# Feed-forward block products: the fifth product's operand added up in the first one's SBUF buffer for three of five double groups, instead of in DRAM

## The chip, the cores and the metric

The kernel runs on one core of a Trainium2 chip. A core has a matrix engine (PE, with its weight loads shown as PEld), a vector engine (DVE), an activation engine (ACT), a general engine (POOL) and a queue engine (SP) that does nothing here but issue transfers. Each engine takes its instructions in program order and waits at semaphores. Transfers run on 16 shared DMA engines: those that SP issues go through one queue (q1 in the profile), those that POOL issues through another (q0). Only POOL issues transfers that add to what lies at their destination.

The metric is the device time of one execution in microseconds, as the median of some runs.

## What is computed

One layer of a decoder over 256 tokens of width 1024: rotary attention in blocks beside an HGRN2 recurrence, a gated merge, cross-attention to 256 memory tokens, and at its end a feed-forward block of hidden width 2816. The change is in how the weights of the last part are brought in:

```python
hn = rmsnorm(h, norm_ffn_g[l])
gu = hn @ w_ffn_in[l]
h = h + (jax.nn.silu(gu[..., :FFN_HIDDEN]) * gu[..., FFN_HIDDEN:]) @ w_ffn_out[l]
...
return rmsnorm(h, final_norm_g)
```

## The kernel before, in words

**Matmuls.** All weights lie in DRAM as units of 128x2048 float32 (1 MB). A unit is loaded into SBUF ("raw"), split by ACT into a rounded part ("hi", two halves of 128x1024) and by DVE into the rest ("lo"), and PE multiplies three times (hi by hi, hi by lo, lo by hi). Up to the feed-forward part `prep` does this (load L254, hi L261, lo L265), two units ahead of PE, with three "raw" buffers that go round; PE takes a unit in `gemm_f` (L338, L339) or `gemm_t` (L317 to L319).

**Feed-forward.** The hidden width has eleven slices of 256 columns. Ten of them are taken as five double groups, q = 1, 3, 5, 7, 9 (slices q and q+1), each with seven products instead of eight, after Strassen's scheme (Winograd's form). The four weight blocks of a group are called 11, 21, 12 and 22. The products, in the order in which PE takes them:

- P1 uses block 11, P2 block 21
- P6 uses 11 + 12 + 22, P7 uses 12 + 22, P5 uses 11 + 12
- P3 uses block 22
- P4 uses 11 + 12 + 21 + 22, up to signs that the tokens' side carries

A product (`ffn_product`, L1143) is 12 matmuls. Between products stand the output matmuls of earlier slices ("O" units, `ffn_out`, 24 matmuls). `FFN_PLAN` is the order of all 48 units. In it a group's P1 to P5 read P1, P2, O, P6, P7, P5 for q = 3, 5 and 7, then follow O, P3, P4 and the next group's P1.

**Where the sums are made.** `block_sums` makes them in DRAM long before, in steps: one step goes by with each matmul unit of the first two thirds, and the table `SUMS` gives the step of each. For each group SP copies a block within DRAM and POOL adds another block to it with an accumulating transfer:

- t3 = 22 (SP, L830), then t3 += 12 (POOL, L819): the operand of P7
- t1 = 11 (SP, L831), then t1 += 12 (POOL): the operand of P5
- t2 = t3 (SP, L834), then t2 += 11 (POOL): the operand of P6

The copy of t3 into t2 must wait for the addition into t3 to land. These transfers are held in program order on SP and POOL (`keep_in_program_order`). SP's loads of the weights of the earlier stages stand in the same row, so whatever SP waits for, the loads behind it wait for too.

P4's operand of groups 3 to 9 is made in another way: P2's block stays in its SBUF buffer (B12 or B6), and once it is split, POOL adds P6's sum to it there (L1413). `operand` then hands the same buffer to P4.

**Feed-forward loads.** `prep_u` brings units in up to four ahead of the one that PE takes: `operand` or `fetch` issues the load (SP, L1388; L1395 for P2's block), `halve` splits it (ACT L1374, DVE L1382). `fetch` takes buffers in the order of `raws`: three "raw" buffers and, from the eleventh load on, B10 and B11 in turn with them ("rawx"). The split parts lie in three hi and three lo buffers and one fixed pair (px), so a unit is split once PE is through with the unit some four places earlier.

Of the kernel before, what the change touches and what calls it, by code (L numbers as in the profile page):

```python
# [12 lines left out]
F32 = mybir.dt.float32  # L13
# [3 lines left out]
ALU = mybir.AluOpType  # L17
# [74 lines left out]
def ffn_plan():  # L92
# [10 lines left out]
    for q in (3, 5, 7):  # L103
# [4 lines left out]

FFN_PLAN = ffn_plan()
DOUBLES = (1, 3, 5, 7, 9)  # L110
PINNED = (5, 6)
FIRST = [0, 4, 1, 2, 3]
SUMS = {1: (0, 4, 2, 6, 10, 13), 3: (7, 9, 8, 11, 17, 20), 5: (13, 15, 16, 18, 26, 28), 7: (22, 25, 29, 31, 32, 34),
        9: (33, 36, 46, 51, 48, None)}
HOME = (36, 38)
T4 = (19, 23)
TURNS = {6: (0,), 10: (1,), 12: (2,), 19: (3,), 21: (4,), 28: (5,), 30: (6,), 38: (7,), 41: (8,)}
# [53 lines left out]
def build(tc, A, out):  # L171
    nc = tc.nc
    V, SC, G, PE, SY = nc.vector, nc.scalar, nc.gpsimd, nc.tensor, nc.sync
    with ExitStack() as ctx:
# [8 lines left out]
        dr = pool("dr", 1, space=bass.MemoryType.DRAM)  # L183
# [3 lines left out]
        def big(tag, name, shape=(128, 8, 256), dt=F32):  # L187
            return bp.tile(list(shape), dt, name=name, tag=tag)
# [31 lines left out]
        made, at = [0], [0]  # L220
# [590 lines left out]
        scr = {}  # L811

        def block(q, name):
            i, kh = {"11": (1, 0), "21": (1, 1), "12": (0, 0), "22": (0, 1)}[name]
            return A["w"][where["T", "wkv_x", 1024 + 512 * (1 - i), kh] if q == "vx" else where["I", q + i, kh]]

        def block_sums():
            def add(t, q, name):
                tc.keep_in_program_order(G.dma_start(t, block(q, name), accum_op=ALU.add, max_dma_last_dim=8192))  # L819

            steps = {}

            def at_step(i, f):
                steps.setdefault(i, []).append(f)

            for q in DOUBLES:
                t1, t2_, t3 = (dr.tile([128, 2048], F32, name="%s_%s" % (z, q)) for z in ("t1", "t2", "t3"))
                scr[q] = {"P5": t1, "P6": t2_, "P7": t3}
                at = SUMS[q]
                at_step(at[0], lambda t=t3, q=q: tc.keep_in_program_order(SY.dma_start(t, block(q, "22"))))  # L830
                at_step(at[2], lambda t=t1, q=q: tc.keep_in_program_order(SY.dma_start(t, block(q, "11"))))  # L831
                at_step(at[1], lambda t=t3, q=q: add(t, q, "12"))
                at_step(at[3], lambda t=t1, q=q: add(t, q, "12"))
                at_step(at[4], lambda t=t2_, t3=t3: tc.keep_in_program_order(SY.dma_start(t, t3)))  # L834
                if q != DOUBLES[-1]:
                    at_step(at[5], lambda t=t2_, q=q: add(t, q, "11"))
                if q == DOUBLES[0]:
                    t4 = dr.tile([128, 2048], F32, name="t4")
                    scr[q]["P4"] = t4
                    at_step(T4[0], lambda t=t4, t2_=t2_: tc.keep_in_program_order(SY.dma_start(t, t2_)))  # L840
                    at_step(T4[1], lambda t=t4, q=q: add(t, q, "21"))
            def home():
                sums["3"] = big("B6", "b22", (128, 2048))
                SY.dma_start(sums["3"], block("vx", "22"))

            at_step(HOME[0], home)
            at_step(HOME[1], lambda: G.dma_start(sums["3"], block("vx", "12"), accum_op=ALU.add))
            for i in range(max(steps) + 1):
                for f in steps.get(i, ()):
                    f()  # L850
                yield 1
# [431 lines left out]
        def last_sum():  # L1283
            tc.keep_in_program_order(G.dma_start(scr[DOUBLES[-1]]["P6"], block(DOUBLES[-1], "11"), accum_op=ALU.add,
                                                 max_dma_last_dim=8192))
# [63 lines left out]


        px = big("P1", "px", (128, 4096), F32R)
        made_u, pair, blk = [0], {}, {}
        homes = itertools.cycle(("B12", "B6"))
        raws = itertools.chain((None,) * 6 + ("B6", None, "B12", None), itertools.cycle(("B10", "B11", None, None, None)))

        PAIRS = [None, None, None, "px", ("B7", "B14"), ("B10", "B11")]

        def halve(raw, n):
            def pin(z):
                if n in PINNED:  # L1360
                    tc.keep_in_program_order(z)

            tags = PAIRS[n] if n < 6 else PAIRS[n % 4 + 2 if n % 4 == 1 else 0]
            if tags == "px":
                hi, lo = px[:, 0:2048], px[:, 2048:4096]
            elif tags:
                hi, lo = (big(tag, name, (128, 2048), F32R) for tag, name in zip(tags, ("hix", "lox")))
            else:
                hi = wh.tile([128, 2048], F32R, name="hi", tag="hi")
                lo = wl.tile([128, 2048], F32R, name="lo", tag="lo")  # L1370
            for c in range(2):
                a = slice(c * 1024, (c + 1) * 1024)
                with tc.issue_after(turned_v[3] if n == 0 else squared[1]) if n == 0 or (n, c) == (3, 1) else nullcontext():
                    pin(SC.activation(hi[:, a], raw[:, a], AF.Copy))  # L1374
            pieces = 2 if n < 3 else 1
            w = 2048 // pieces
            for c in range(pieces):
                a = slice(c * w, (c + 1) * w)
                with ExitStack() as then:
                    for ins in behind.get(n, ()) if (n, c) != (2, 1) else (added[1],):  # L1380
                        then.enter_context(tc.issue_after(ins))
                    pin(V.tensor_tensor(lo[:, a], raw[:, a], hi[:, a].bitcast(F32), op=ALU.subtract))  # L1382
            return hi, lo
# [8 lines left out]
        def operand(q, name):  # L1392
            if name == "P2" and q != DOUBLES[0]:
                blk[q] = big(next(homes), "b21", (128, 2048))
                tc.keep_in_program_order(SY.dma_start(blk[q], block(q, "21")))  # L1395
                return blk[q]
            if name == "P4" and q in blk:
                return blk.pop(q)
            return fetch(scr[q][name] if name in scr[q] else block(q, {"P1": "11", "P2": "21", "P3": "22"}[name]))
# [3 lines left out]
        def prep_u(upto):  # L1403
            while made_u[0] <= min(upto, len(units) - 1):
                n = FIRST[made_u[0]] if made_u[0] < len(FIRST) else made_u[0]
                if n == 20:
                    SY.dma_start(gfin, A["gfin"].to_broadcast([128, 1024]))
                made_u[0] += 1
                u = units[n]
                raw = operand(u[1], u[2]) if u[0] == "P" else fetch(A["w"][where[u]])  # L1410
                pair[n] = halve(raw, n)
                if u[0] == "P" and u[1] in blk and u[2] == "P2":
                    G.dma_start(raw, scr[u[1]]["P6"], accum_op=ALU.add)  # L1413

# [181 lines left out]
        for n in range(4, len(units) - 2):  # L1596
# [6 lines left out]
            u = units[n]  # L1603
# [123 lines left out]
```

## Time and profile before

| what | before |
|---|---|
| median of 3 runs | 592.38 us (592.34 to 592.53) |
| the profiled execution: time | 592.17 us |
| the profiled execution: span of its instructions | 590.2 us |
| its granted TensorE clock | 0.998 |
| PE busy | 582.3 us |
| DVE busy | 452.5 us |
| ACT busy | 389.5 us |
| POOL busy | 122.5 us |
| moved by transfers | 161.92 MB |

The span is the time from the first instruction to the last; 1.97 us of the profiled execution's time lie around it. "Busy" counts an engine's instructions but not its waits and not the issuing of transfers. In lists of waits, "A <- B" says that A stood still until B was done. For a transfer the profile gives the time from its issue to its landing.

### The profile page before, as it was taken

Reading aid. Unit: us, or ns where it says so; the run is one execution under the profiler, and the core shown is the slowest. Engines: PE = TensorE matmul, PEld = TensorE weight load, DVE = VectorE, ACT = ScalarE, POOL = GpSimd, SP = SyncE. Lnnn points to the kernel's source line nnn. Section 1 sums busy time; section 2 is a strip of 40 time slices with the busy share of each in tenths; the row PEclk is TensorE's granted clock in tenths of the full one; section 3 lists DMA queues with packets and bytes.
Section 4 is the critical chain, followed back from the end, with each engine's and each line's share of the span. In section 5 each row is a group of like instructions: output and inputs, shape, how many; then the busy total and the mean of one; then the engine's idle time right before and its main releaser. Section 6 shows DMA issues by size and latency. Waiting matters only on the chain.

```text
span 590.2 us, 9030 instructions
## 1 busy us (share of the span) xinstructions
PE 582.3 (99%) x3474; PEld 487.9 (83%) x3474; DVE 452.5 (77%) x638; ACT 389.5 (66%) x638; POOL 122.5 (21%) x139
## 2 busy tenths in 40 slices
PE   9999999999999999999999999999999999999995
PEld 6888888888888888888888888888888888888884
DVE  6598967789858775858868785987878887877943
ACT  7795646555677566657548676776858676776743
POOL 2897300243301430003202332200000000000003
PEclk9999999999999999999999999999999999999999
DMA  9877997489996799899976986886989969796601
GB/s 337 339 273 290 274 343 310 144 277 354 325 308 243 210 299 333 264 403 276 256 242 184 372 268 237 212 283 245 366 289 294 408 180 421 200 418 190 236 1 71
DMA packets 22586, 161.92 MB, mean 274 GB/s; under 512 B 2832, under 2 KB 3472, under 8 KB 5392
## 3 DMA queue, kind: packets, MB, share of 16 engines
q1 hardware_dynamic: 18368, 135.35, 58.1%
q0 software_dynamic: 3456, 25.17, 21.8%
q10 hardware_dynamic: 720, 0.84, 0.4%
q8 instruction: 27, 0.44, 0.3%
q14 instruction: 15, 0.12, 0.1%
HBM read 160.29 MB, written 34.60 MB: 330 GB/s over the span
## 4 chain that ended last, share of the span: by engine, by line
PE 92%; DVE 3%; ACT 1%; issue 1%; POOL 1%; DMA 1%; DVEq 0%; POOLq 0%; ACTq 0%
PE psf L338 13%; PE pqA L1143 11%; PE pst L317 9%; PE pst L318 8%; PE pst L319 8%; PE psf L339 6%; PE pqF L1143 6%; PE acc L317 3%; PE acc L319 3%; PE acc L318 3%; PE pqB L1143 3%; DVE lo L265 2%; PE psg L593 1%; PE pso L318 1%; PE pso L319 1%
## 5 line engine op out<-in xcount | busy, mean ns | idle before, releaser
L265 DVE TENSOR_TENSOR lo<-raw,hi 128x1024 fp32r<-128x1024 f32 (+1 forms) x126 | 156.8, 1262 | 39.4 <-ACT hi L261 39.1
L261 ACT ACTIVATE hi<-raw 128x1024 fp32r<-128x1024 f32 (+1 forms) x126 | 126.5, 1027 | 56.6 <-PE pst L319 25.9
L338 PE MATMUL psf<-XX,hi 128*128 128x512 f32 x192 | 68.5, 401 | 0.0
L317 PE MATMUL pst<-hi,XX 128*128 128x512 f32 x160 | 63.7, 398 | 0.0
L319 PE MATMUL pst<-hi,XX 128*128 128x512 f32 x160 | 62.5, 390 | 0.0
L318 PE MATMUL pst<-lo,XX 128*128 128x512 f32 x160 | 62.4, 390 | 0.0
L339 PE MATMUL psf<-XX,lo 128*128 128x256 f32 x192 | 54.0, 281 | 0.0
L1382 DVE TENSOR_TENSOR lo<-raw,hi 128x2048 fp32r<-128x2048 f32 (+1 forms) x19 | 37.0, 1951 | 10.6 <-ACT hi L1374 10.5
L338 PEld LDWEIGHTS psf<-XX,hi 128*128 128x128 f32 x192 | 36.1, 188 | 8.7
L1374 ACT ACTIVATE hi<-raw 128x1024 fp32r<-128x1024 f32 x32 | 32.0, 1051 | 7.3 <-PE acc L319 5.3
L339 PEld LDWEIGHTS psf<-XX,lo 128*128 128x128 f32 x192 | 36.4, 189 | 0.0
L317 PEld LDWEIGHTS pst<-hi,XX 128*128 128x128 f32 x160 | 30.1, 188 | 7.3 <-issue 1.0
L319 PEld LDWEIGHTS pst<-hi,XX 128*128 128x128 f32 x160 | 30.0, 188 | 6.4
L318 PEld LDWEIGHTS pst<-lo,XX 128*128 128x128 f32 x160 | 30.1, 188 | 5.8
L1382 DVE TENSOR_TENSOR lo<-rawx,hi 128x2048 fp32r<-128x2048 f32 x12 | 27.5, 2288 | 7.6 <-ACT hi L1374 7.6
L1413 POOL DMA_DIRECT2D b<-t x4 | 3.5, 884 | 123.4 <-DVE fu L1476 88.1
L1374 ACT ACTIVATE hi<-rawx 128x1024 fp32r<-128x1024 f32 x24 | 24.1, 1050 | 4.8 <-DMA rawx<-w 1.8
L1143 PE MATMUL pqA<-hi,SS 128*128 128x512 f32 x80 | 26.4, 391 | 0.0
L317 PE MATMUL acc<-hi,hids 128*128 128x512 f32 x62 | 24.5, 395 | 0.0
L319 PE MATMUL acc<-hi,hids 128*128 128x512 f32 x62 | 24.2, 390 | 0.0
L318 PE MATMUL acc<-lo,hids 128*128 128x512 f32 x62 | 24.2, 390 | 0.0
L338 PE MATMUL psf<-H,hi 128*128 128x512 f32 x64 | 22.8, 400 | 0.0
(470 smaller groups left out, 1506.2 us busy)
## 6 DMA issues: line engine op xcount, KB each, us to landing
raw<-w SPq DMA_DIRECT2D x74, 1024.0 KB, 7.8
t<-w POOLq DMA_DIRECT2D x16, 1024.0 KB, 12.8
raw<-t SPq DMA_DIRECT2D x12, 1024.0 KB, 7.9
rawx<-w SPq DMA_DIRECT2D x10, 1024.0 KB, 7.5
b<-w SPq DMA_DIRECT2D x6, 1024.0 KB, 8.8
b<-w POOLq DMA_DIRECT2D x4, 1024.0 KB, 9.2
rawx<-t SPq DMA_DIRECT2D x4, 1024.0 KB, 7.8
b<-t POOLq DMA_DIRECT2D x4, 1024.0 KB, 9.4
```

Of the source, the lines that this page charges most:

```text
L261: SC.activation(hi[:, a], raw[:, a], AF.Copy)
L265: V.tensor_tensor(lo[:, a], raw[:, a], hi[:, a].bitcast(F32), op=ALU.subtract)
L317: PE.matmul(ps, xh, h, start=first, stop=False)
L318: PE.matmul(ps, xh, l, start=False, stop=False)
L319: PE.matmul(ps, xl, h, start=False, stop=last)
L338: PE.matmul(ps, w[0][:, k, a], X2[:, :, k], start=k == 0, stop=False)
L339: PE.matmul(ps[:, 0], w[1][:, k, a], X2[:, 0, k], start=False, stop=k == 7)
L593: PE.matmul(pss[c][t], z[:, k, t * 128:(t + 1) * 128], ws[c][0][:, k], start=z is Xh and k == 0, stop=False)
L1143: PE.matmul(ps, x[k], z[:, k], start=first and k == 0 and i == 0, stop=k == 3 and i == 2, skip_group_check=not first)
L1374: pin(SC.activation(hi[:, a], raw[:, a], AF.Copy))
L1382: pin(V.tensor_tensor(lo[:, a], raw[:, a], hi[:, a].bitcast(F32), op=ALU.subtract))
L1413: G.dma_start(raw, scr[u[1]]["P6"], accum_op=ALU.add)
```

## The change

For q = 3, 5 and 7 (`GROWN`), t1 is no longer made in DRAM: one copy of SP and one addition of POOL fall away for each. The first product's block 11 is loaded into buffer B10 (for q = 3, 5, 7 and 9). Once it is split for P1, POOL issues a transfer that adds block 12 to it in that buffer, and P5 takes its operand from there, with no load of its own. For q = 1 and q = 9, P5's operand is made in DRAM as before. B10 leaves the turn of the other loads: from the eleventh on they have four buffers instead of five.

`SUMS` is written in another order of columns. For q = 1 and 9 its steps are the same. For q = 3 the copy of t3 into t2 moves from step 17 to 11 and the addition to t2 from 20 to 17; for q = 5 from 26 to 18 and from 28 to 26; for q = 7 the copy from 32 to 31.

```diff
+GROWN = (3, 5, 7)
...
-SUMS = {1: (0, 4, 2, 6, 10, 13), 3: (7, 9, 8, 11, 17, 20), 5: (13, 15, 16, 18, 26, 28), 7: (22, 25, 29, 31, 32, 34),
-        9: (33, 36, 46, 51, 48, None)}
+SUMS = {1: (0, 4, 10, 13, 2, 6), 3: (7, 9, 11, 17), 5: (13, 15, 18, 26), 7: (22, 25, 31, 34),
+        9: (33, 36, 48, None, 46, 51)}
...
-                t1, t2_, t3 = (dr.tile([128, 2048], F32, name="%s_%s" % (z, q)) for z in ("t1", "t2", "t3"))
-                scr[q] = {"P5": t1, "P6": t2_, "P7": t3}
+                t2_, t3 = (dr.tile([128, 2048], F32, name="%s_%s" % (z, q)) for z in ("t2", "t3"))
+                scr[q] = {"P6": t2_, "P7": t3}
                 at = SUMS[q]
                 at_step(at[0], lambda t=t3, q=q: tc.keep_in_program_order(SY.dma_start(t, block(q, "22"))))
-                at_step(at[2], lambda t=t1, q=q: tc.keep_in_program_order(SY.dma_start(t, block(q, "11"))))
                 at_step(at[1], lambda t=t3, q=q: add(t, q, "12"))
-                at_step(at[3], lambda t=t1, q=q: add(t, q, "12"))
-                at_step(at[4], lambda t=t2_, t3=t3: tc.keep_in_program_order(SY.dma_start(t, t3)))
+                if q not in GROWN:
+                    t1 = scr[q]["P5"] = dr.tile([128, 2048], F32, name="t1_%s" % q)
+                    at_step(at[4], lambda t=t1, q=q: tc.keep_in_program_order(SY.dma_start(t, block(q, "11"))))
+                    at_step(at[5], lambda t=t1, q=q: add(t, q, "12"))
+                at_step(at[2], lambda t=t2_, t3=t3: tc.keep_in_program_order(SY.dma_start(t, t3)))
                 if q != DOUBLES[-1]:
-                    at_step(at[5], lambda t=t2_, q=q: add(t, q, "11"))
+                    at_step(at[3], lambda t=t2_, q=q: add(t, q, "11"))
...
-        raws = itertools.chain((None,) * 6 + ("B6", None, "B12", None), itertools.cycle(("B10", "B11", None, None, None)))
+        raws = itertools.chain((None,) * 6 + ("B6", None, "B12", None), itertools.cycle(("B11", None, None, None)))
...
+            if name == "P1" and q != DOUBLES[0]:
+                early[q] = big("B10", "b11", (128, 2048))
+                SY.dma_start(early[q], block(q, "11"))
+                return early[q]
+            if name == "P5" and q in GROWN:
+                return early[q]
...
                 pair[n] = halve(raw, n)
+                if u[0] == "P" and u[1] in GROWN and u[2] == "P1":
+                    G.dma_start(raw, block(u[1], "12"), accum_op=ALU.add)
```

The rows below show what the change moves. They name a transfer by its tiles, out<-in ("w" is the weights' array), and in brackets the semaphores it waits for: DMASW stands for the landing of one of POOL's transfers, DMAHW for that of one of SP's, the rest for engines.

The first place is SP's row in the stage of the first projections, some 120 to 165 us into the span. Before:

```order
L830 DMA t3_5_723<-w 16x16384
L254 DMA raw_1599<-w 128x2048 [waits DMAHW7_49,DMAHW3_49,DVE_49]
L254 DMA raw_1673<-w 128x2048 [waits DMAHW0_49,DVE_49]
L254 DMA raw_1790<-w 128x2048 [waits DMAHW1_49,DVE_49]
L831 DMA t1_5_721<-w 16x16384 [waits DMAHW6_49]
L254 DMA raw_1835<-w 128x2048 [waits DMAHW3_49,DVE_49]
L834 DMA t2_3_719<-t3_3_720 16x16384 [waits DMASW2_49]
L254 DMA raw_1880<-w 128x2048 [waits DMAHW4_49,DVE_49]
L254 DMA raw_1935<-w 128x2048 [waits DMAHW5_49,DMAHW2_49,DVE_49]
L840 DMA t4_717<-t2_1_715 16x16384 [waits DMASW4_49]
L254 DMA raw_2051<-w 128x2048 [waits DMAHW7_49,DVE_49]
```

And the same stretch of SP's row with the change:

```order
L831 DMA t3_5_721<-w 16x16384 [waits DMAHW1_49]
L837 DMA t2_3_718<-t3_3_719 16x16384 [waits DMASW2_49]
L255 DMA raw_1595<-w 128x2048 [waits DMAHW6_49,DVE_49]
L255 DMA raw_1669<-w 128x2048 [waits DMAHW7_49,DVE_49]
L255 DMA raw_1786<-w 128x2048 [waits DMAHW5_49,DMAHW0_49,DVE_49]
L255 DMA raw_1830<-w 128x2048 [waits DMAHW3_49,DVE_49]
L255 DMA raw_1875<-w 128x2048 [waits DMAHW4_49,DVE_49]
L255 DMA raw_1930<-w 128x2048 [waits DMAHW5_49,DVE_49]
L843 DMA t4_717<-t2_1_714 16x16384 [waits DMAHW1_49,DMASW3_49]
L837 DMA t2_5_720<-t3_5_721 16x16384 [waits DMAHW2_49,DMASW4_49]
L255 DMA raw_2046<-w 128x2048 [waits DMAHW6_49,DVE_49]
```

The copy t2<-t3 of group 3 now stands ahead of four loads that it stood behind (raw_1595 is the load that was raw_1599), and that of group 5 ahead of raw_2046; the copy into t1 is gone.

The second place is SP's row in the feed-forward part, for the loads of group 5 (some 452 to 474 us into the span): P3 of group 3, then P1, O, P6, P7 and P5 of group 5. Before:

```order
L1388 DMA rawx_4616<-w 128x2048 [waits DMAHW7_49,DMAHW2_49,DVE_49]
L1388 DMA raw_4658<-w 128x2048 [waits DMAHW3_49,DVE_49]
L1388 DMA raw_4713<-w 128x2048 [waits DMAHW4_49,DVE_49]
L1388 DMA raw_4735<-t2_5_722 128x2048 [waits DMAHW0_49,DMASW2_49,DVE_49]
L1388 DMA rawx_4764<-t3_5_723 128x2048 [waits DMAHW6_49,DMAHW1_49,DVE_49]
L1388 DMA rawx_4790<-t1_5_721 128x2048 [waits DMAHW2_49,DVE_49]
```

With the change:

```order
L1391 DMA rawx_4606<-w 128x2048 [waits DMAHW4_49,DVE_49]
L1391 DMA raw_4704<-w 128x2048 [waits DMAHW7_49,DVE_49]
L1391 DMA raw_4726<-t2_5_720 128x2048 [waits DMAHW0_49,DMAHW1_49,DMASW0_49,DVE_49]
L1402 DMA b11_4648<-w 128x2048 [waits DMASW1_49,DVE_49]
L1391 DMA raw_4755<-t3_5_721 128x2048 [waits DMAHW5_49,DMAHW2_49,DVE_49]
L1391 DMA rawx_4817<-w 128x2048 [waits DMAHW6_49,DMAHW3_49,DVE_49]
```

P1's load (b11) moves behind those of O and P6, since its buffer comes free only when P5 of group 3 has been split; P5's load is gone and the next O's (rawx_4817) stands in its place.

The third place is POOL's row from the start of the feed-forward part on, where three transfers become six. With the change (those of L1424 are the three of L1413 before):

```order
L1422 DMA b11_4413<-w 128x2048 [waits DMAHW2_49,DVE_49,Pool_49]
L1424 DMA b21_4464<-t2_3_718 128x2048 [waits DMASW2_49,DMAHW3_49,DVE_49,DMAHW5_49,Activation_49,Pool_49]
L1422 DMA b11_4648<-w 128x2048 [waits DMASW3_49,DMAHW1_49,DMASW1_49,DVE_49]
L1424 DMA b21_4681<-t2_5_720 128x2048 [waits DMAHW0_49,DVE_49]
L1422 DMA b11_4879<-w 128x2048 [waits DMAHW7_49,DMASW3_49,DVE_49]
L1424 DMA b21_4911<-t2_7_722 128x2048 [waits DMASW6_49,DMAHW0_49,DMASW2_49,DVE_49]
```

One addition of block 12 is put ahead of each of these three; a fourth addition of L1413, for group 9, follows behind them in both kernels.

More of the change, by code (lines that the diff above doesn't have):

```diff
@@ L1351, in build @@
         px = big("P1", "px", (128, 4096), F32R)
-        made_u, pair, blk = [0], {}, {}
+        made_u, pair, blk, early = [0], {}, {}, {}
         homes = itertools.cycle(("B12", "B6"))
-        raws = itertools.chain((None,) * 6 + ("B6", None, "B12", None), itertools.cycle(("B10", "B11", None, None, None)))
+        raws = itertools.chain((None,) * 6 + ("B6", None, "B12", None), itertools.cycle(("B11", None, None, None)))
         PAIRS = [None, None, None, "px", ("B7", "B14"), ("B10", "B11")]
```

## The prediction

> **What bounds the kernel now.** I read the page first, then PE's waits, then the stages that the change touches. From the page: span, busy times, PE's share in 40 slices, the two queues of transfers, and the chain of work that ended last.
>
> ```profile
> span 590.2 us, 9030 instructions
> ...
> PE 582.3 (99%) x3474; PEld 487.9 (83%) x3474; DVE 452.5 (77%) x638; ACT 389.5 (66%) x638; POOL 122.5 (21%) x139
> ...
> PE   9999999999999999999999999999999999999995
> ...
> q1 hardware_dynamic: 18368, 135.35, 58.1%
> q0 software_dynamic: 3456, 25.17, 21.8%
> ...
> PE 92%; DVE 3%; ACT 1%; issue 1%; POOL 1%; DMA 1%; DVEq 0%; POOLq 0%; ACTq 0%
> ```
>
> PE is busy in every slice but the last, and the chain is PE for 92%. PE's list of waits has two rows:
>
> ```profile
> PE warm L411 <- PEq L1718: 0.8, 1, 0.8
> PE psg L593 <- ACT hi L261: 0.7, 1, 0.7
> ```
>
> Both are at the opening. After it PE waits for nothing that the list shows. Where the chain leaves PE, one look tells how much waiting that is:
>
> ```profile
> 203.62 4.81 issue
> ...
> 221.50 0.58 ACT tat L1002
> ...
> 222.12 0.50 PE pst L317
> ```
>
> PE stood for ACT at 222.12, yet at most for the 0.6 us of that last ACT step; and the chain that ends there, which runs over ACT, DVE and POOL from 184 us on, has 4.8 us in it from 203.6 on in which its engine waited for nothing that the profile shows, so the work ahead of that has some 4.8 us in hand. In the feed-forward part, one window of 110 us:
>
> ```profile
> 440.00:550.00 110.00, 110.00 (x500) 91.09 (x499) 88.49 (x65) 78.81 (x99) 3.54 (x4) 1.00 0.87 305
> ```
>
> The columns are the stretch, its length, then busy PE, PEld, DVE, ACT and POOL, the granted clock, the DMA engines' busy share and GB/s. PE is busy for all of it at full clock, and the DMA engines are 0.87 busy. So the kernel is bound by PE, and an edit that leaves PE's 3474 matmuls in their order can gain only what PE waits today: after the opening, less than 0.6 us at that place. It can lose whatever new wait it makes.
>
> **The change part by part.** *Removed.* Three copies and three additions in DRAM. A 1.05 MB transfer of q1 takes 0.581 x 590.2 / 135.35 x 1.05 = 2.7 us of all 16 DMA engines, one of q0 takes 0.218 x 590.2 / 25.17 x 1.05 = 5.4 us. The first half is relieved of 3 x 8.1 = 24 us of DMA work. As PE does not wait for transfers there, that is worth 0.
>
> *Moved: t2<-t3 of group 3.* SP now waits for the addition into t3 ahead of the load that follows.
>
> ```profile
> 119.09 0.49 SPq L830 DMA_DIRECT2D t<-w  x1
> ...
> 122.57 0.34 SPq L254 DMA_DIRECT2D raw<-w  x1
> ...
> L819 POOL DMA_DIRECT2D t<-w x1: 804/804/804, 119.9 to 119.9; - x1
> DMA to landing us min/median/max: 14.1/14.1/14.1
> ```
>
> POOL issued this addition at 119.9, behind vector work of its own that the change leaves alone, and it landed 14.1 us later, at 134.0. In the changed row SP stands at the copy from 119.6 on, and the load that left at 122.57 leaves only after that landing. So up to 11.5 us are lost on that load. What does it have in hand?
>
> ```profile
> L254 SPq DMA_DIRECT2D raw<-w x1: 337/337/337, 122.6 to 122.6; - x1
> DMA to landing us min/median/max: 11.7/11.7/11.7
> ...
> 136.12 1.06 ACT L261 ACTIVATE hi<-raw 128x1024 fp32r<-128x1024 f32 x1 [2.22 <-PE psf L338]
> 139.42 1.21 DVE L265 TENSOR_TENSOR lo<-raw,hi 128x1024 fp32r<-128x1024 f32 x1
> 150.13 0.50 PE L317 MATMUL pst<-hi,XX 128*128 128x512 f32 x1
> ```
>
> It landed at 134.3, ACT began to split it at 136.1, DVE ended at 140.6, and PE takes it at 150.1: 9.5 us in hand, and a split takes 4.5 us from ACT's start. The two ends: if the addition again takes 14.1 us and the load again 11.7, it lands at 134.0 + 0.5 + 11.7 = 146.2, the split ends at 150.7, and PE waits 0.6 us. At the other end the load that shared the DMA engines with the addition is now behind it; the fastest of the fifteen additions sets that end:
>
> ```profile
> L819 POOL DMA_DIRECT2D t<-w x15: 787/832/1191, 53.6 to 370.2; - x15
> DMA to landing us min/median/max: 8.7/12.8/22.0
> L254 SPq DMA_DIRECT2D raw<-w x60: 327/328/439, 7.7 to 378.6; - x60
> DMA to landing us min/median/max: 4.7/8.1/15.2
> ```
>
> With 8.7 us and then the median load of 8.1 it lands at 137.2, and PE waits 0. I take about 12 us for the addition (a little under the median, since fewer loads run beside it) and 8.1 for the load, whose rivals are one copy and one load: landing 140.5, split by 145, 5 us ahead of PE. ACT and DVE run some 4 us late for a while, of which ACT wins back the 2.2 us that it had stood idle. Cost 0, ends 0 and 0.6.
>
> *Moved: t2<-t3 of group 5.* It stands right behind the copy into t4 and waits for an addition that POOL issued at 155.0:
>
> ```profile
> 164.26 0.33 SPq L254 DMA_DIRECT2D raw<-w  x1
> ...
> L819 POOL DMA_DIRECT2D t<-w x1: 787/787/787, 155.0 to 155.0; - x1
> DMA to landing us min/median/max: 14.2/14.2/14.2
> ...
> 177.13 1.06 ACT L261 ACTIVATE hi<-raw 128x1024 fp32r<-128x1024 f32 x1 [0.48 <-DMA raw<-w]
> 179.96 1.22 DVE L265 TENSOR_TENSOR lo<-raw,hi 128x1024 fp32r<-128x1024 f32 x1
> 191.90 0.48 PE L317 MATMUL pst<-hi,XX 128*128 128x512 f32 x1
> ```
>
> With 14.2 us SP is free at 169.2, and the load that left at 164.26 is 5 us late; with the two transfers of t1 gone from 130 to 177 us it is likelier 2 us. ACT waited for this very load, so a delay is felt at once by ACT, but the split ended at 181.2 and PE came at 191.9: 10.7 us in hand. DVE's next steps, which stand behind this split, feed the chain that ends at 222; of 5.4 us late (169.2 + 0.5 - 164.3) the 4.8 us in hand there leave 0.6. Cost 0, ends 0 and 0.6; I take 0, since 2 us lie nearer and well within the 4.8.
>
> *Added: three additions into B10.* Their nearest rows are the four that add to P2's block, and the load in P1's new place:
>
> ```profile
> L1413 POOL DMA_DIRECT2D b<-t x4: 862/880/915, 449.6 to 540.4; - x4
> DMA to landing us min/median/max: 8.5/9.4/10.0
> ...
> L1388 SPq DMA_DIRECT2D raw<-t x1: 327/327/327, 460.5 to 460.5; - x1
> DMA to landing us min/median/max: 8.3/8.3/8.3
> ...
> 468.86 2.00 ACT L1374 ACTIVATE hi<-raw 128x1024 fp32r<-128x1024 f32 x2
> 470.89 2.29 DVE L1382 TENSOR_TENSOR lo<-raw,hi 128x2048 fp32r<-128x2048 f32 x1 [0.26 <-ACT hi L1374]
> 485.21 2.01 ACT L1374 ACTIVATE hi<-rawx 128x1024 fp32r<-128x1024 f32 x2 [0.28 <-ACT hi L1374]
> 487.77 2.28 DVE L1382 TENSOR_TENSOR lo<-rawx,hi 128x2048 fp32r<-128x2048 f32 x1
> 496.49 2.72 PE pqA L1143 x12
> ```
>
> In group 5, P1's load takes the third place, at 460.5, and lands at 468.8, just when ACT came to it (468.86). DVE ends P1's split at 473.2; the addition then has until 485.2, when ACT comes to P5's operand: 12.0 us against 8.5 to 10.0. PE comes at 496.5, and P5's split took 4.8 us, so it could land as late as 491.6, 18.4 us after its issue. Behind P1's addition on POOL stands P2's. Its first packets wait for P1's last, but P4, which needs it, is PE's seventh unit after P2. POOL has 3.54 us of work in 110, so its three issues of 0.9 us cost 0. Cost 0, ends 0 and 3.6 us for each group if an addition into SBUF took the 22.0 us of the slowest one into DRAM (473.2 + 22.0 + 4.8 - 496.5); I take the row of its own kind.
>
> *DMA engines in this stage.* Three loads of 2.7 us become additions of 5.4: 8.1 us more, where 0.13 x 110 = 14 us are free. It still fits, at 0.94.
>
> **Sum.** 592.17 us for the profiled execution, plus 0, 0 and 0, less perhaps 0.1 of the 0.6 at 222: 592.1; the median before stands 0.2 above that execution, so 592.3.
>
> **Rivals.** *Slower: SP is held at the t3 addition until PE starves.* PE waits once that addition takes longer than 150.1 - 4.5 - 8.1 - 0.5 - 119.9 = 17.1 us; at the 22.0 us of the slowest row it waits 4.9 us, giving 597. Against it: this one is first in its queue, and 22.0 was the third of three issued within 4 us. For it: the loads of this stretch took up to 15.2 us, and DVE's late work also feeds other steps. At a few us late the time is about 594 to 595. *Slower: the feed-forward part runs out of DMA time.* 0.94 busy leaves 6 us; if P5 lands after 491.6, each us costs one, in three groups; 3.6 each would give 603. The trace speaks against it with 8.5 to 10.0. The Trainium skill's page DMA: Bandwidth & Descriptors, SWDGE vs HWDGE vs iDMA, says that a DMA engine takes turns between its internal queues, so POOL's additions and SP's loads slow each other; the trace agrees so far as loads beside an addition took 8.3 us. *Faster: the relief of 24 us is felt.* It needs a PE that is not full. The window above gives PEld 91.09 of 110 = 83%, with PE waiting for nothing; a weight load to each matmul is what full streaming looks like there, so I give it little: 591. The Trainium skill's page Perfetto Trace Analysis, Identifying the Most-Contended Engine, says that matmul busy time misleads and that weight-load time should be used; by it a sixth of the time would be open, but the same 83% stands where nothing is waited for. *The change does nothing:* if SP's row were the old one; the rows above show that it is not.
>
> **How the numbers follow.** PE still full, 0.80, at 591.6 to 593; SP held, 0.12, at 594 to 597; DMA time short, 0.04, at 594 and up; relief felt, 0.04, at about 591. A measurement of this kernel tells about 0.2%, 1.2 us, from no change. That makes faster 0.04, same 0.80, slower 0.16. The range goes from 591.6, the 0.6 at 222 gained in full, to 594.4: both moves at their upper ends make 593.5, and the mild part of the first rival reaches to 594.4, so that about 0.15 is left out above and 0.04 below.
>
> **What would show it.** PE's waits after the opening still empty, and the window's PE column full, show the sum right. SP's copy at L837 issued between 129 and 134 with the next load right behind, and that load's split done before PE comes, show the first move right; a PE row waiting for DVE near 150 or 192 shows the first rival. In the feed-forward part, additions at L1422 of 8.5 to 10 us, a DMA share near 0.94, and ACT not waiting more than 1 us for P5's operand show the third; a PE row waiting for DVE in three groups shows the second rival. A faster PE with no wait removed would show that I read its fullness wrongly.

## The result, and the profile after

| what | before | changed |
|---|---|---|
| median | 592.36 us (591.88 to 592.81, 9 runs) | 595.94 us (593.73 to 597.52, 9 runs) |
| ratio to before, 95% interval | | 1.0053 [1.0037, 1.0069] |
| profiled execution: time, span | 592.17, 590.2 us | 596.62, 594.6 us |
| its granted TensorE clock | 0.998 | 0.995 |
| PE busy | 582.3 us | 585.2 us |
| moved by transfers | 161.92 MB | 155.63 MB |

The change makes the kernel 0.5% slower, and its times spread over 3.8 us where those of before spread over 0.9. Before, PE's list of waits ended with the opening. This is the whole list of the changed kernel:

```profile
PE lv L729 <- DVE amx L926: 2.3, 1, 2.3
PE warm L412 <- PEq L1729: 0.8, 1, 0.8
```

One new row, at lv. The units are counted in the order in which they are loaded; unit 24 is the one whose load now stands right behind group 3's copy. The start of PE on each unit, set beside that of before, says how much was lost by then in the profiled executions: unit 24 starts 0.30 us later, unit 25 4.28, unit 26 4.49, and the difference stays there to the end. So the whole loss lies at 156 to 162 us, and the feed-forward part has none. The chain that leads to it, from the timelines of SP, ACT, DVE and PE of the changed kernel (start, duration, engine, line, operation, out<-in, and in brackets the idle time before and its releaser):

```profile
119.08 0.49 SPq L831 DMA_DIRECT2D t<-w  x1
131.69 0.48 SPq L837 DMA_DIRECT2D t<-t  x1
132.27 4.00 SPq L255 DMA_DIRECT2D raw<-w  x3
...
141.73 1.06 ACT L262 ACTIVATE hi<-raw 128x1024 fp32r<-128x1024 f32 x1 [7.70 <-DMA raw<-w]
...
142.82 1.23 DVE L266 TENSOR_TENSOR lo<-raw,hi 128x1024 fp32r<-128x1024 f32 x1 [5.23 <-ACT hi L262]
...
157.73 0.28 DVE L926 CUSTOM_DVE_ANT_0 ap<-as,cst 128x128 f32<-128x128 f32 x1
...
158.42 3.61 PE L729 MATMUL lv<-QK 128*128 128x128 f32 x16 [2.25 <-DVE amx L926]
161.68 0.65 PE L318 MATMUL pst<-hi,XX 128*128 128x512 f32 x1
```

SP stands at group 3's copy t2<-t3 (L837) until the addition into t3 lands at 131.68. The load of unit 24 leaves at 132.27 instead of 122.57 and lands at 141.65. ACT and DVE wait for it. PE has unit 24 in time (split at 145.51, taken at 150.43), but at 156.17 it comes to lv, a 16-matmul step of the recurrence (`level`). lv needs a PSUM bank of the pool that holds the four score tiles "as", and the first of these comes free only when DVE has taken its maxima (ap, amx), at 158.4. The last row is PE's first product of unit 25. The rows of ap, lv and that product before:

```profile
153.50 0.28 DVE L923 CUSTOM_DVE_ANT_0 ap<-as,cst 128x128 f32<-128x128 f32 x1
...
155.70 1.95 PE L728 MATMUL lv<-QK 128*128 128x128 f32 x16
...
157.40 0.48 PE L317 MATMUL pst<-hi,XX 128*128 128x512 f32 x1
```

There the bank was free 0.69 us after 153.50 (the distance from ap to lv in the changed kernel), at 154.19: it had **1.5 us in hand**, and DVE came 4.2 us late.

DVE had no way to make this up. Windows of before and then of the changed kernel (columns as in the prediction):

```profile
134.00:142.00 8.00, 8.00 (x56) 6.90 (x56) 8.00 (x11) 3.00 (x5) 3.42 (x3) 1.00 1.03 293
142.00:150.00 8.00, 8.00 (x94) 6.76 (x88) 7.30 (x10) 4.80 (x9) 3.96 (x5) 1.00 1.11 416
150.00:156.00 6.00, 6.00 (x31) 4.91 (x28) 6.00 (x22) 1.68 (x2) 2.34 (x4) 1.00 0.90 270
```

```profile
140.00:142.00 2.00, 2.00 (x14) 1.55 (x12) 0.00 (x0) 0.27 (x1) 0.00 (x0) 1.00 0.99 410
142.00:150.00 8.00, 8.00 (x93) 6.96 (x96) 7.18 (x9) 7.00 (x12) 3.19 (x3) 1.00 0.70 253
150.00:158.00 8.00, 6.17 (x36) 4.53 (x28) 8.00 (x14) 1.18 (x2) 1.99 (x3) 1.00 0.95 233
```

Before, the fifth column (DVE) is busy for 21.3 of 22 us. Afterwards it stands idle at 140 to 142.8 for the load, and is then full to 158. It begins unit 24's split 5.4 us late (142.82 for 137.40) and comes to the maxima 4.2 us late: with 0.7 us of slack in 22 it could win back little.

In the profiled execution the wait is 2.25 us and the loss 4.4. The rest is in the clock (last but two column):

```profile
155.00:156.20 1.20, 1.17 (x6) 0.63 (x4) 1.20 (x3) 0.00 (x0) 0.00 (x0) 1.00 0.90 259
156.20:158.40 2.20, 0.00 (x0) 0.00 (x0) 2.20 (x8) 0.00 (x0) 0.51 (x1) 1.00 1.01 357
158.40:158.70 0.30, 0.28 (x2) 0.28 (x3) 0.30 (x3) 0.00 (x0) 0.30 (x2) 0.89 1.50 437
158.70:162.00 3.30, 3.30 (x17) 3.30 (x17) 1.69 (x12) 2.58 (x8) 2.18 (x3) 0.50 1.48 511
162.00:166.00 4.00, 4.00 (x19) 3.29 (x18) 2.80 (x11) 4.00 (x14) 0.00 (x0) 0.99 0.60 162
```

Right behind the wait the granted clock is 0.50 for some 3.4 us, which costs half of that, 1.7 us: lv takes 3.61 us where it took 1.95. The sum, 0.3 (PE already later at unit 24) + 2.25 + 1.7 = 4.3, is what unit 25 shows.

The feed-forward part, in a window moved by the 4.4 us, and the row of the new additions:

```profile
444.40:554.40 110.00, 110.00 (x501) 91.03 (x500) 88.31 (x65) 78.94 (x99) 6.13 (x7) 1.00 0.91 296
```

```profile
L1422 POOL DMA_DIRECT2D b<-w x3: 858/868/912, 450.9 to 509.0; - x3
...
DMA to landing us min/median/max: 7.9/8.1/8.1
```

PE is full, the DMA engines are 0.91 busy (forecast 0.94), and the additions land in 7.9 to 8.1 us (forecast 8.5 to 10.0). The three into P2's block that follow them on POOL took 10.8 to 13.4 us where they had taken 8.9 to 10.0, and no wait is put down to them.

### The profile page after: what moved, and what is told of

It is laid out like the page before. It is cut to its first block, busy times and chain, and to the rows that moved or that the text cites. A ratio compares the mean times of both kernels' runs of the same rounds, so it can differ in the third digit from the quotient of the medians.

```text
span 594.6 us, 9027 instructions
## 1 busy us (share of the span) xinstructions
PE 585.2 (98%) x3474; PEld 489.7 (82%) x3474; DVE 451.1 (76%) x638; ACT 390.0 (66%) x638; POOL 124.9 (21%) x139
## 2 busy tenths in 40 slices
DMA packets 22058, 155.63 MB, mean 262 GB/s; under 512 B 2736, under 2 KB 3376, under 8 KB 5296
## 4 chain that ended last, share of the span: by engine, by line
PE 91%; DVE 3%; DMA 2%; ACT 2%; issue 1%; POOL 1%; DVEq 0%; ACTq 0%
PE pqA L1146 11%; PE psf L339 11%; PE pst L318 9%; PE pst L320 9%; PE pst L319 9%; PE pqF L1146 6%; PE psf L340 5%; PE acc L318 3%; PE acc L320 3%; PE acc L319 3%; PE pqB L1146 3%; DMA raw<-w 2%; PE psg L594 1%; PE pso L320 1%; PE pso L319 1%; PE pso L318 1%
## 5 line engine op out<-in xcount | busy, mean ns | idle before, releaser
L266 DVE TENSOR_TENSOR lo<-raw,hi 128x1024 fp32r<-128x1024 f32 (+1 forms) x126 | 155.1, 1249 | 45.8 <-ACT hi L262 45.5
L262 ACT ACTIVATE hi<-raw 128x1024 fp32r<-128x1024 f32 (+1 forms) x126 | 126.6, 1027 | 58.4 <-PE pst L320 24.2
L1385 DVE TENSOR_TENSOR lo<-raw,hi 128x2048 fp32r<-128x2048 f32 (+1 forms) x21 | 41.6, 1985 | 13.5 <-ACT hi L1377 13.5
L1377 ACT ACTIVATE hi<-raw 128x1024 fp32r<-128x1024 f32 x36 | 36.0, 1051 | 9.2 <-PE acc L320 6.2
L1385 DVE TENSOR_TENSOR lo<-b,hi 128x2048 fp32r<-128x2048 f32 x12 | 27.5, 2289 | 9.2 <-ACT hi L1377 9.2
L1377 ACT ACTIVATE hi<-b 128x1024 fp32r<-128x1024 f32 x24 | 24.1, 1052 | 9.4 <-DMA b<-w 4.7
L320 PE MATMUL acc<-hi,hids 128*128 128x512 f32 x62 | 24.2, 390 | 0.0
L339 PE MATMUL psf<-M,hi 128*128 128x512 f32 x64 | 22.7, 398 | 0.0
## 6 DMA issues: line engine op xcount, KB each, us to landing
b<-t POOLq DMA_DIRECT2D x4, 1024.0 KB, 11.6
```

The source lines that it names most:

```text
L320: PE.matmul(ps, xl, h, start=False, stop=last)
L339: PE.matmul(ps, w[0][:, k, a], X2[:, :, k], start=k == 0, stop=False)
```

## The experiments

**Theory A**: the loss is group 3's early copy, by SP's hold, DVE's late queue and the bank of lv. **Theory B**: it is in the feed-forward part. **Theory C**: it is group 5's early copy.

**1. One part of the change at a time.** The first three are the changed kernel with other steps in `SUMS`, the fourth the kernel before with one copy early.

Group 3 late:

```diff
-SUMS = {1: (0, 4, 10, 13, 2, 6), 3: (7, 9, 11, 17), 5: (13, 15, 18, 26), 7: (22, 25, 31, 34),
+SUMS = {1: (0, 4, 10, 13, 2, 6), 3: (7, 9, 17, 20), 5: (13, 15, 18, 26), 7: (22, 25, 31, 34),
```

Group 5 late, and both late:

```diff
+SUMS = {1: (0, 4, 10, 13, 2, 6), 3: (7, 9, 11, 17), 5: (13, 15, 26, 28), 7: (22, 25, 31, 34),
+SUMS = {1: (0, 4, 10, 13, 2, 6), 3: (7, 9, 17, 20), 5: (13, 15, 26, 28), 7: (22, 25, 31, 34),
```

The kernel before with group 3 early:

```diff
-SUMS = {1: (0, 4, 2, 6, 10, 13), 3: (7, 9, 8, 11, 17, 20), 5: (13, 15, 16, 18, 26, 28), 7: (22, 25, 29, 31, 32, 34),
+SUMS = {1: (0, 4, 2, 6, 10, 13), 3: (7, 9, 8, 11, 11, 17), 5: (13, 15, 16, 18, 26, 28), 7: (22, 25, 29, 31, 32, 34),
```

> The changed kernel with only group 3's copy t2<-t3 and its addition put back to steps 17 and 20. Theory A (the early copy of group 3 holds SP until the addition into t3 lands; DVE then runs some 4 us late, the scores' PSUM banks come free late, and PE waits 2.25 us for one at lv and runs some 2 us more under a lower clock): 592.3 us within 0.5, ratio to before 1.000, no PE wait at lv, lv at 155.7 to 156.2, granted clock 1.00 there. Theory B (the additions into B10 or the turn of four buffers in the feed-forward part cost it): about 596, ratio 1.005. Theory C (the hold of group 5's copy at 159 to 171 us costs it): about 596.

> The changed kernel with only group 5's copy t2<-t3 and its addition put back to steps 26 and 28; group 3's copy stays early. Theory A: like the changed kernel, 594 to 597.5 us, ratio 1.003 to 1.007, with the PE wait at lv of about 2.2 us. Theory B: about 596 as well. Theory C: 592.3, and no PE wait at lv.

> The changed kernel with the copies and additions of groups 3 and 5 both back at their old steps, so that only the feed-forward part of the change and the missing t1 transfers are left. Theory A: 592.3 us within 0.5, ratio 1.000. Theory B: about 596, ratio 1.005. Theory C: 592.3. If the relief of 24 us of DMA work were felt: 591.5 or less.

> The kernel before, with t1 still made in DRAM and no addition into SBUF, and only group 3's copy t2<-t3 moved to step 11 and its addition to step 17. Theory A: as slow as the changed kernel or more, 594 to 598 us, ratio 1.003 to 1.009, with a PE wait for DVE at lv of 2 us or more (t1's transfers still run beside the load, so its landing is at 142 or later). Theory B and C: 592.4, ratio 1.000, no wait at lv.

| kernel | median us | ratio to before [95%] | PE wait at lv |
|---|---|---|---|
| group 3 late | 592.24 | 0.9996 [0.9986, 1.0005] | none |
| group 5 late | 593.88 | 1.0025 [1.0014, 1.0037] | 1.83 us |
| both late | 592.08 | 0.9991 [0.9982, 0.9999] | none |
| before, group 3 early | 599.16 | 1.0105 [1.0087, 1.0122] | 3.48 us |

A holds, B and C fall: putting group 3's copy back removes the loss, and that copy alone, in the kernel before, makes it, larger still and 1.2 us above the range expected (t1's transfers then run beside the held load, which takes 11.6 us and lands at 143.77). "Group 5 late", though, was 2 us lower than the changed kernel's 595.94 and just under the 594 expected, so it was run again (part 3). PE's list of waits with group 3's copy early in the kernel before:

```profile
PE lv L728 <- DVE amx L923: 3.5, 1, 3.5
PE warm L411 <- PEq L1718: 0.8, 1, 0.8
PE psf L338 <- DVE rz L330: 0.6, 1, 0.6
```

**2. The bank, the clock, the place of the copy, and the slack.** Four edits. Lv's tiles come from the other pool:

```diff
-                    ps = bank("lv", (128, 4, 128))
+                    ps = mm.tile([128, 4, 128], F32, name="lv", tag="mm")
```

Products that fill PE's wait stand ahead of lv:

```diff
+                fill = mm.tile([128, 512], F32, name="fill", tag="mm")
+                [PE.matmul(fill[:, 0:128], KS[:, 2 * (h % 8)], QP[:, 2 * (h % 8) + 1], start=True, stop=True) for h in range(10)]
```

Group 3's copy stands two loads further on:

```diff
-SUMS = {1: (0, 4, 10, 13, 2, 6), 3: (7, 9, 11, 17), 5: (13, 15, 18, 26), 7: (22, 25, 31, 34),
+SUMS = {1: (0, 4, 10, 13, 2, 6), 3: (7, 9, 15, 17), 5: (13, 15, 18, 26), 7: (22, 25, 31, 34),
```

And in the kernel before DVE does one subtraction twice:

```diff
-                    V.tensor_tensor(lo[:, a], raw[:, a], hi[:, a].bitcast(F32), op=ALU.subtract)
+                    for _ in range(2 if (i, c) == (25, 0) else 1): V.tensor_tensor(lo[:, a], raw[:, a], hi[:, a].bitcast(F32), op=ALU.subtract)
```

> The changed kernel with its early copies as they are; only lv's two PSUM tiles of 128x4x128 come from the other pool of four banks (that of the projections' sums), so that lv does not wait for the scores' banks. Theory A1 (PE stands for the scores' bank only): the load still leaves at 132.3, ACT and DVE are still some 4 us late, but PE has no wait at lv or one below 0.5 us, and the time is 592.3 to 592.8, ratio 1.000 to 1.001. Rival A2 (PE would next stand for another of DVE's late results, such as the split of units 25 or 26 or a projection's bank): the wait moves by some us and the time stays at 594 to 597.

> The changed kernel with ten more products of 128x128 (5/4 of lv's own work, results not read) ahead of lv, which need no late bank; at full clock they take about 2.2 us, as long as PE waits. If the lower clock behind the wait comes from PE standing still (theory A with a clock part): the wait turns into work, the granted clock stays at 1.00 from 156 to 162, lv takes 1.8 us, and the time is 594.3 to 594.9, that is 1.5 us faster than the changed kernel's median. If the lower clock has another cause (the work itself, or chance): lv still takes 3.6 us, and the time is 596 to 597.

> The changed kernel with group 3's copy t2<-t3 two loads further on in SP's row (step 15; its addition at 17 as before). The loads of units 24 and 25 leave as in the kernel before; the addition into t3 lands at about 132 to 134, and SP reaches the copy at about 126 to 128, so the hold is 5 to 8 us, and it falls on the load of unit 26 and those behind it. Theory A: DVE is not late at the scores (ap at 153.5 to 154.5), no wait at lv, 592.3 within 0.5. Rival (any hold of SP in this stretch starves PE some units on): 594 or more, with a PE wait after 162.

> The kernel before with no transfer moved; DVE repeats one subtraction of 128x1024 (1.2 us, first half of unit 25's lo) ahead of the scores. It makes DVE 1.1 to 1.2 us late there. Theory A says the scores' banks have some 1.6 us in hand at lv: no wait or one below 0.3 us, and 592.4 within 0.5. If PE had nothing in hand there: a wait of about 1.2 us, and with the lower clock 593.5 to 595.

| kernel | median us (lowest to highest) | ratio to before [95%] |
|---|---|---|
| lv's other bank | 593.88 (592.84 to 596.39) | 1.0033 [1.0020, 1.0046] |
| wait filled | 595.16 (594.3 to 598.73) | 1.0055 [1.0036, 1.0074] |
| copy two loads on | 592.32 (591.9 to 593.65) | 1.0000 [0.9991, 1.0009] |
| one subtraction twice | 592.55 (592.2 to 592.81) | 0.9998 [0.9988, 1.0008] |

*Copy two loads on* is as forecast: SP still waits for the addition, until 133.74, but units 24 and 25 have left, and what stands behind has time. The hold is not the cost; the load behind it is. *One subtraction twice* in the kernel before costs nothing, but it is a weak test of the 1.5 us in hand: at the maxima DVE was only 0.4 us later than before (ap at 153.92, not 153.50), and lv came 1.65 us behind ap instead of 2.20, so that 0.55 of the 1.5 us was used.

*Lv's other bank* is nearer to rival A2, a little under its 594: in the profiled run lv starts at 155.86 without a wait, yet the median is 1.5 us over before. What comes next is in that run's rows:

```profile
161.86 1.05 ACT L262 ACTIVATE hi<-raw 128x1024 fp32r<-128x1024 f32 x1
162.81 1.05 ACT L730 ACTIVATE ATS<-lv 128x512 f32<-128x512 f32 x2
...
163.43 0.50 PE L318 MATMUL pst<-hi,XX 128*128 128x512 f32 x1 [0.18 <-ACT ATS L730]
```

ACT copies lv out only behind the exponentials, which wait for DVE's late maxima; unit 26's sums now need that bank. The wait moved 5 us on; here it is 0.18 us. This profiled run was the fastest of twelve (its held load landed early, at 139.26), so the median's 1.5 us was still to be shown.

*Wait filled*: the clock stays up in the profiled run. PE's rows and its windows:

```profile
155.86 2.39 PE L724 MATMUL fill<-QK 128*128 128x128 f32 x20
158.09 2.04 PE L729 MATMUL lv<-QK 128*128 128x128 f32 x16
```

```profile
156.00:158.00 2.00, 2.00 (x21) 2.00 (x19) 2.00 (x8) 0.00 (x0) 0.45 (x1) 1.00 0.96 348
158.00:160.00 2.00, 2.00 (x20) 1.99 (x19) 1.97 (x16) 0.93 (x1) 2.00 (x4) 1.00 0.97 315
```

With PE busy through the stretch, lv takes 2.04 us at clock 1.00: in the changed kernel the lower clock came from PE standing still. The median of 595.16 is above the 594.3 to 594.9 forecast, and four of ten runs are over 596. In the profiled one PE loses a further 1.7 us in the cross-attention, at 367 to 386 us by the times of the kernel before; the profile puts 0.4 us of it down to a wait for DVE (at xT). That place lost 1.3 us in one other profiled run as well (the repeat of the changed kernel), and none in the rest. What sets it off is open. One of the ten runs, at 598.46 us, had a mean clock of 0.994; where its clock fell is not on record.

**3. The same on one chip again.** In the runs so far in which PE waited at lv, lv came 16.8 us after the held load's landing, whatever that was. Three more runs test it.

> The changed kernel itself, once more, on the same chip as the next two. Two readings of the first runs: (1) PE reaches lv at about 156.2, and the scores' bank comes free 16.8 us after the held load of unit 24 lands (16.77 in the changed kernel, 16.78 with group 5 back, 16.76 in the kernel before with group 3 early), so a landing at 139.4 or earlier costs nothing and each us later costs one us, and a lower clock adds 1.7 to 2.0 us in runs where it comes. By it this profile shows lv at its unit-24 landing + 16.8, and the runs lie at 593 to 597.5, median about 595. (2) The wait is fixed: lv at 158.4 whatever the landing.

> The changed kernel with only group 5's copy and addition back, again. If group 5's early copy costs nothing of its own: the same median as the changed kernel on this chip within 0.8 us, and the difference seen before (593.9 against 595.9) was between chips or by chance of the landing. If it costs 1.5 to 2 us on top of group 3's: this one is that much below the changed kernel again, and its median is at 593.5 to 594.

> The changed kernel with lv's tiles from the other pool of banks and group 5's copy and addition back at 26 and 28; group 3's copy stays early. If the 1.5 us left in the run with lv's other bank were group 5's: 592.4. If they are the next late result of the same hold (unit 26's sums need the banks that lv now takes, and ACT copies lv out only behind the exponentials that wait for DVE's late maxima): 593.3 to 594.5, and the profile shows PE waiting at the first product of unit 26 for ACT's copy of lv, with a start at the landing of unit 24 + 24.2 (163.43 less 139.26 in the first such run), if that is later than 163.2.

| kernel | median us | ratio to before [95%] |
|---|---|---|
| changed, again | 594.66 | 1.0039 [1.0024, 1.0055] |
| group 5 late, again | 594.93 | 1.0045 [1.0029, 1.0062] |
| lv's other bank, group 5 late | 594.38 | 1.0033 [1.0021, 1.0046] |

Group 5's early copy costs nothing that these runs can tell: on one chip its two versions are 0.3 us apart, and with group 3 late 0.2 us (592.24 and 592.08 in part 1). The first difference of 2 us did not come again: from the first set of runs to the second the changed kernel went from 595.94 to 594.66 and group 5 late from 593.88 to 594.93. How much of that is the chip and how much the chance of the landings stays open. The landings, with what followed, in all the profiled runs so far with group 3's early copy and lv's bank as it was (us):

| profiled run | unit 24 landed | lv started | distance | wait | clock 0.50 for |
|---|---|---|---|---|---|
| group 5 late, again | 139.88 | 156.66 | 16.78 | 0.61 | 0 |
| group 5 late | 140.80 | 157.58 | 16.78 | 1.83 | 3.4 |
| wait filled | 141.29 | 158.09 | 16.80 | filled | 0 |
| changed | 141.65 | 158.42 | 16.77 | 2.25 | 3.4 |
| changed, again | 141.91 | 158.67 | 16.76 | 2.31 | 3.4 |
| before, group 3 early | 143.77 | 160.53 | 16.76 | 3.48 | 6.8 |

Reading (1) holds to 0.04 us. (In the row "wait filled" lv follows the filling products without a gap, so the row shows only that the bank was free by then; but DVE's first maxima came 16.1 us behind the landing there as in the five others.) PE gets to lv at about 156.1 (155.7 to 156.4, and 157.05 in the last row, where it had already waited 0.6 us at psf), so a landing up to 139.3 is free, and each us beyond it costs one us of wait, and the lower clock where that comes. Group 5 late, again, landed 0.6 us beyond that and waited 0.6; its time was 593.26 us.

For lv's other bank the moved wait came where forecast: landing 140.28 + 24.2 = 164.48, and PE's row is

```profile
164.48 0.64 PE L318 MATMUL pst<-hi,XX 128*128 128x512 f32 x1 [1.82 <-ACT ATS L730]
```

**4. Two splits off DVE, on POOL.** If DVE's gapless queue makes the 16.8 us, a shorter queue must shorten them.

```diff
-                    V.tensor_tensor(lo[:, a], raw[:, a], hi[:, a].bitcast(F32), op=ALU.subtract)
+                    (G if (i, c) in ((25, 1), (26, 1)) else V).tensor_tensor(lo[:, a], raw[:, a], hi[:, a].bitcast(F32), op=ALU.subtract)
```

> The changed kernel with the early copies as they are; two of the six subtractions of 128x1024 that stand on DVE between the held load's landing and the scores' maxima (second halves of units 25 and 26) are done by POOL. Theory: DVE has no gap from the landing on, so its queue alone sets the 16.8 us from landing to lv; with 1.34 and 1.13 us of it gone (the distance to the next start, in the changed kernel) lv comes 14.3 us after the landing of unit 24, or when PE gets there (156.2), whichever is later: for landings of 139.3 to 141.9 no PE wait at lv, granted clock 1.00, 592.3 to 593. Rival (DVE's queue is not what sets it, but ACT's or the landing of units 25 and 26, or POOL is now late with kT): lv at landing + 16 or more or another PE wait, 594 to 597.

598.51 us, ratio 1.0102 [1.0085, 1.0118]: a miss, and the worst version but one. Rows of DVE and of POOL in that run:

```profile
149.64 3.27 DVE L899 TENSOR_TENSOR ra<-rz,tables 128x512 f32<-128x512 f32 x1
...
156.99 2.31 DVE L899 TENSOR_TENSOR ra<-rz,tables 128x512 f32<-128x512 f32 x1
159.22 0.68 DVE L900 TENSOR_TENSOR rb__1718<-rz,tables 128x512 f32<-128x512 f32 x1
```

```profile
149.68 2.67 POOL L266 TENSOR_TENSOR lo<-raw,hi 128x1024 fp32r<-128x1024 f32 x1
...
155.42 3.32 POOL L266 TENSOR_TENSOR lo<-raw,hi 128x1024 fp32r<-128x1024 f32 x1
```

DVE's ra takes 3.27 and 2.31 us beside POOL's subtractions, where the same shape (see rb below it) takes 0.68: 4.2 us added for 2.5 removed. The maxima came 2.1 us later for the same landing (141.61; lv at 160.50, a distance of 18.9). A longer queue gave a longer distance, so the theory wasn't hurt, but the edit did not test what it was meant to.

**5. DVE's queue shorter by order alone.** Unit 26's two subtractions move behind the first maxima; PE needs them only at 162.9. Group 5 is late, since with it early SP's order would have moved too.

```diff
-                with tc.issue_after(scaled[1]) if STREAM[i] == "P5" and c else nullcontext():
+                with tc.issue_after(scaled[1]) if STREAM[i] == "P5" and c else tc.issue_after(maxima[0]) if i == 26 else nullcontext():
                     V.tensor_tensor(lo[:, a], raw[:, a], hi[:, a].bitcast(F32), op=ALU.subtract)
...
-                V.tensor_scalar(nm, mx, -0.125, None, op0=ALU.mult)
+                maxima.append(V.tensor_scalar(nm, mx, -0.125, None, op0=ALU.mult).ins)
```

> Group 3's early copy as in the changed kernel, group 5's copy and addition back at 26 and 28, and the two subtractions of unit 26 (128x1024 each), which PE needs only at 162.9, moved on DVE from ahead of the scores' maxima to behind those of the first four. Nothing else moves on DVE and PE. Theory (DVE's queue without a gap sets the time from the held load's landing to lv): the queue is 2 x 1.13 = 2.3 us shorter, so lv comes 14.5 us after the landing of unit 24 or when PE gets there at 156.2; with landings of 139.3 to 141.9 the PE wait at lv is 0 to 0.2 us, the granted clock stays at 1.00, and the median is 592.2 to 593. Rival (the landing itself, ACT, or the units' own splits starve PE): lv still 16.8 us behind the landing, 593.9 to 595 as in the two runs with group 5 back.

592.37 us, ratio 1.0004 [0.9995, 1.0013], with group 3's copy as early as in the changed kernel and the load landing at 141.05, where by 16.8 us lv could only have started at 157.85:

```profile
155.05 0.28 DVE L926 CUSTOM_DVE_ANT_0 ap<-as,cst 128x128 f32<-128x128 f32 x1
...
155.74 2.05 PE L729 MATMUL lv<-QK 128*128 128x128 f32 x16
```

lv starts 14.7 us behind the landing, still right behind the maxima (0.69 us after ap), but PE had come to it only 0.12 us earlier, and the clock stays at 1.00 there. Shortened by these two subtractions, DVE's row let lv start 2.1 us sooner. So the queue that stood on DVE between the late load and the maxima is what carried the lateness to PE.

No version beats the kernel before by a margin worth having. The best, both copies late, is 0.9991 [0.9982, 0.9999].

## Why the prediction was wrong

- *PE is the bound; an edit can gain next to nothing and lose whatever wait it makes.* Right, and it is how the result came about.
- *Removed: 24 us of DMA work, worth 0.* Right within 0.2%: with both copies late the kernel has the relief and the additions of the feed-forward part, and it stands at 0.9991 [0.9982, 0.9999].
- *Moved: t2<-t3 of group 3, "Cost 0, ends 0 and 0.6".* **This step failed.** Its transfers were well forecast: an addition of about 12 us (11.76), a landing at 140.5 (141.65), unit 24 split 5 us ahead of PE (4.9). What failed is the sentence "ACT and DVE run some 4 us late for a while, of which ACT wins back the 2.2 us that it had stood idle". I asked only when PE takes that unit, and never which other results stand behind its split in DVE's row and when PE takes those. The row has rz, ra, rb, QK and the splits of two more units, and then the maxima that free lv's bank, with 1.5 us in hand and not 9.5. And ACT's idle time was no help: the late engine that mattered was DVE, at 21.3 busy of 22 us. With my own landing of 140.5 the wait would have been 140.5 + 16.8 - 156.1 = 1.2 us already. The sign that I had named for this step was therefore no sign: SP's copy left at 131.69, the load right behind it, and the split was done before PE came, all as forecast, and the loss came all the same.
- *Rival "SP is held at the t3 addition until PE starves".* It had a chance of 0.12 and 594 to 597, and the median lies there. The right mechanism with the wrong point. I priced it by unit 24 (an addition of over 17.1 us) and put "DVE's late work also feeds other steps" behind it as a remark. By lv's bank the point is a landing at 139.3, so with the same 8.1 us for the load an addition of 10.8 us; those of the runs with the early copy took 11.3 to 12.4 us, so the point was passed nearly every time.
- *Moved: t2<-t3 of group 5, cost 0.* The cost is right, the lateness was mis-sized. I took 2 us. With group 3 late the load behind the copy left at 169.13, 4.9 us later than before, yet it landed at 176.71 where it had landed at 177.11, since it took 7.6 us instead of 12.8. In the changed kernel it left at 171.97 and landed at 181.26, about as late as PE itself by then. No PE wait follows in either, and late and early versions are equal on one chip.
- *Added: three additions into B10, cost 0.* Right: 7.9 to 8.1 us, group 5's P1 load in 9.97 (I took 8.3), no PE wait in the stage, DMA engines 0.91 busy. ACT came to the first P5 operand with 0.52 us to wait. (The upper end of 3.6 us for each group comes out at 3.5.)
- *The clock* was in no term. In the profiled run PE's pause cost 1.7 us more than its length. Of the changed kernel's nine runs, the four with a mean clock of 0.997 or 0.998 took 593.7 to 594.7 us and the five with 0.994 to 0.996 took 595.9 to 597.5, so the dip goes with about half of the loss and much of the spread. This is an indication only: runs of the kernel before have 0.996 to 0.999 at about 592 us, and in the repeat a run with 0.998 took 597.33 us.

## What to carry to other kernels

When a step makes an in-order engine late, list everything behind it in that engine's row and take the smallest slack of all; the unit that the late transfer feeds is only the first on the list, and a PSUM bank held by a late reader counts as a result. A late engine wins back time only where its own busy column has gaps. And a copy that must wait for a transfer in a shared queue is placed by what stands behind it: two loads further on, the same wait was free.

## What the runs showed of the hardware

**PE pauses of 1.8 us and more came with half clock for 3.4 us.** Pauses of 1.83, 2.25 and 2.31 us at lv were each followed by a stretch of 3.4 us at granted clock 0.50, and so was the 1.82 us wait of the last row in part 3. The pause of 3.48 us in the kernel before with group 3 early came with twice that:

```profile
157.00:159.50 2.50, 0.05 (x1) 0.00 (x0) 2.50 (x5) 0.00 (x0) 0.00 (x0) 1.00 0.96 262
159.50:166.00 6.50, 5.47 (x21) 5.08 (x22) 4.19 (x24) 4.46 (x16) 3.82 (x5) 0.50 0.98 292
```

The length does not simply grow with the pause: the longest, 4.23 us in the run with two splits on POOL, came with 3.4 us again (160.1 to 163.5). A pause of 0.61 us brought none. Nor does the stretch begin at a fixed distance: it began 0.2 us after PE's restart in the changed kernel, 1.4 us after it in the repeat, and 0.4 and 1.0 us ahead of it in the two longest pauses. The Trainium skill's page TensorE: Matmul & The Clock Gate, Part 1: The HAM clock gate, describes half rate set by a free-running activity window of about 3.4 us; length, rate and shifting phase agree. Its rule of thumb, no PE-idle gaps of more than about 3.4 us, is too mild here: 1.8 us were enough. In the 3.4 us before each stretch PE had been idle for 1.8 to 3.4 us, over half. Some runs with group 3's copy early had a mean clock of 0.998; whether their pauses were shorter or fell across two windows no run here shows.

**DVE stood beside POOL.** A DVE operation of 0.68 us with two SBUF inputs took 3.27 us while POOL subtracted for 2.67. The Trainium skill's page GPSIMD Engine Reference, Specifications, says that POOL shares its SBUF interfaces with VectorE, with contention for DVE instructions of two SBUF inputs; the trace agrees, and shows that DVE's operation ended only after POOL's did, by 0.56 us both times.
